# A depthwise convolution moved whole to TensorE, and GpSimd's products and splits moved to VectorE

## The chip, the core and the metric

One core of one Trainium2 chip runs the whole program. Its engines work side by side, each through its own queue in order: TensorE (PE in the profile; its weight loads are PEld), VectorE (DVE), ScalarE (ACT), GpSimd (POOL) and SyncE (SP), which issues most DMAs. The metric is the time of one execution in device microseconds.

## The reference

A network of four blocks, 512 tokens (T) by 1024 features (D = 8 tiles of 128), in float32. The change is in the first half of the first block, "even": an input projection of 5120 columns whose parts feed an S5 layer (a state space recurrence) and a convolution branch, each gated, then an output projection. The convolution branch:

```python
def conformer_conv(val, gate, w_dw, b_dw, ln_g, ln_b, w_pw, b_pw):
    h = val * sigmoid(gate)
    h = depthwise causal convolution of h with w_dw, 31 taps for each channel, + b_dw
    h = silu(layer_norm(h, ln_g, ln_b))
    return h @ w_pw + b_pw
```

(shortened to its steps). The S5 layer expands its poles into powers, keeps 64 groups of states and runs a recurrence over the tokens; the kernel does it by chunks of 8 tokens.

## The kernel before, in words

Features lie on the 128 partitions, the 512 tokens on the free axis. The program is six stages; `stage_even` is the first, from 0 to about 735 us of the trace. Each product is of float32 operands split into a high and a low part (`K.split`: the high part by ScalarE, line L227, the low part by a subtraction, L230, on VectorE unless `eng` names another engine) and takes three passes (`K.passes`, L271, L272, L273). A block of `K.linear`, 128 output columns, loads its weights (`wraw`), splits them into `whi` and `wlo`, and multiplies 8 tiles in three passes, 24 products of 128x512.

Within `stage_even` a scheduler sets the order on each engine from its own model of the times; the order in the source only limits it. The work is:

- The first 8 blocks of the input projection give S5 its inputs. `s5_tables` prepares S5's poles on VectorE meanwhile. The weights' low parts of these 8 blocks are made by GpSimd (`eng=nc.gpsimd`).
- `s5_group`, 8 calls with 4 rounds each: a round makes two sums of two products (`t1`, `t2` into `Gm`; `w1`, `w2` into `w1`), of which VectorE makes the first product and the sum (L685, L687, L693, L695) and GpSimd the second product (L686, L694). TensorE uses them (L700, L701, L709) and ScalarE copies the states into `H`.
- `s5_scan`, 63 steps of four operations on VectorE (L743 to L746); `s5_chunks` (L731) and `s5_outputs` (L761, L763).
- For each of 8 channel tiles `conv(j)`: a gate block (`g`, sigmoid into `sg`), a value block (`v`), `hb` = value times `sg` (L842), and the convolution of the 31 taps into `c`, which GpSimd adds to `acc` and sends to `cv_dr`. Tiles 0 to 3 multiply each tap on ScalarE (L853) and add on GpSimd (L854). Tiles 6 and 7 use a fused multiply and add on VectorE (L860), after the scan. Tiles 4 and 5 run on TensorE (`conv_pe`): the tap's weights become diagonal matrices (`dgh`, `dgl`, by VectorE, L825), and each tap is three products of 128x512 with `hb` shifted, 93 for a tile.
- 16 blocks with silu go to `z_dr`. Then S5's gelu and GLU (8 blocks, `ya`), the layer norm of the convolution, the pointwise layer (8 blocks) and the output projection (8 blocks over 16 tiles).

`CONV_ORDER` lists in which order the tiles and the two halves of the 16 silu blocks stand in the source.

Of the kernel before, what the change touches and what calls it, by code (L numbers as in the profile page):

```python
# [13 lines left out]
F32 = mybir.dt.float32  # L14
# [3 lines left out]
AF = mybir.ActivationFunctionType  # L18
OP = mybir.AluOpType
# [11 lines left out]
# ---------------------------------------------------------------------------  # L31
# host side: layouts only
# ---------------------------------------------------------------------------
# [7 lines left out]
def _blocks_tok(w):  # L41
    """Blocks for products with tokens on the output partitions: [n/256, k half, 128, 4*256]."""
    k, n = w.shape
    return np.ascontiguousarray(
        w.reshape(2, 4, 128, n // 256, 256).transpose(3, 0, 2, 1, 4)
    ).reshape(n // 256, 2, 128, 1024)
# [7 lines left out]
class Layout:  # L54
    """Named columns of the packed per-feature vectors."""
# [16 lines left out]
def host_layout(i):  # L72
# [30 lines left out]
    # block 2  # L103
# [17 lines left out]
    # block 3  # L121
# [23 lines left out]
# ---------------------------------------------------------------------------  # L145
# device side
# ---------------------------------------------------------------------------
# [4 lines left out]
class Ctx:  # L152
# [50 lines left out]
    # -- psum ------------------------------------------------------------  # L203
    def banks(self, es, **split):
        """Share the 8 banks among tags; the tiles of one tag are handed out in order."""
# [14 lines left out]
    # -- exact operand splits ---------------------------------------------  # L220
    def split(self, hi, lo, x, scale=None, eng=None):
        """eng: the engine of lo, or the engines of hi and lo."""
# [18 lines left out]
    def weights(self, src, kt=KT, eng=None, raw=None, pool=None):  # L241
        """One block of up to 128 output columns: [128, kt, 128], split."""
# [8 lines left out]
    def fetch(self, w, blocks, more=(), own=False):  # L251
        """Weights of the first products of the next stage; those of more not split yet.

        own: in a pool of their own, which the next stage closes.
        """
# [10 lines left out]
    def passes(self, ps, terms, first=True, last=True):  # L266
        """terms: (lhs hi, lhs lo, rhs hi, rhs lo); first, last: where the accumulation group starts and ends."""
# [7 lines left out]
    def linear(self, w, blocks, xh, xl, epi, kt=KT, eng=None, front=0, tail=0):  # L275
        """outT[n, t] for each 128-column block of w; epi(j, psum); eng splits the weights.

        The first and the last blocks (front, tail) take one half of the tokens after the other.
        The last ones have epi(j, psum, tokens) and are left to the function returned, of the tokens.
        """  # L280
# [34 lines left out]
    def linear_steps(self, w, blocks, xh, xl, epi):  # L315
        """linear() in steps of KT products of a block."""
# [9 lines left out]
    def linear_tok(self, w, blocks, xh, xl, epi, eng=None):  # L326
        """out[t, n]: tokens on partitions; epi(j, t-pair, psum [128, 2, 256])."""
# [14 lines left out]
    # -- statistics over features ------------------------------------------  # L342
    def colsum(self, s):
        """Sum over partitions, on every partition."""
        ps = self.ax_ps()[:, :s.shape[1]]
        self.nc.tensor.matmul(ps, self.ones, s, start=True, stop=True)
        return ps

    def exp_ln(self, after=None):
        """Load the table set that serves both Exp and Ln."""  # L350
# [3 lines left out]
    def rsqrt(self, *args, load=True, **kw):  # L354
        """out = (scale * ps + eps) ** -0.5, or max(ps, eps) ** -0.5; one Newton step on exp(-ln/2)."""
# [26 lines left out]
    def scratch(self, k, ts, tag):  # L382
        """Room for what is worked out of tile k of x: at the end of a stage, what the stage leaves unused."""
# [13 lines left out]
    def sumsq_ps(self, ps, x, k, ts):  # L397
        """ps accumulates the sum of squares over the features of KT tiles, on every partition."""
# [10 lines left out]
    # -- the ends of stages, in steps between which the halves of the tokens take turns -------  # L409
    def rms_pre(self, g):  # L410
        """What a stage that begins with an RMS norm does with x: its split, scaled by rstd * g."""
# [11 lines left out]
    def modulate_pre(self, scale, shift):  # L423
        """What a stage that begins with a modulation does with x: the split of xt * scale + shift."""
# [10 lines left out]
    def enter(self, xt, pre):  # L435
        """The operands of a stage's first products, unless the stage before has left them."""
# [11 lines left out]
    def leave(self, xt, sums, rest, post, pre, dead, mu=None, first=()):  # L448
        """rest(tokens) and the steps of post(tokens) end a stage, pre begins the next."""
# [18 lines left out]
    def rms_post(self, y, acc, xt, g, sums=None):  # L468
        """xt += rms(y) * g; sums[tokens] = sum of squares of the new xt."""
# [23 lines left out]
class Small:  # L493
    """Arithmetic on small float32 tiles [128, 64]."""
# [88 lines left out]
CONV_POOL = (0, 1, 2, 3)  # L583
CONV_PE = (4, 5)
CONV_ORDER = (0, 1, 6, (0, 8), 2, 3, 7, 4, 5, (8, 16))


def s5_tables(K, pool, R8, J8):
    """Discretised poles, their powers with the signs of each half of the partitions, B bar.

    Partitions are (h, n): h = 0 holds real parts of the states, h = 1 imaginary parts.
    """
# [6 lines left out]
    with K.tc.tile_pool(name="s5sm", bufs=1, side="right", reuse_waits="tile") as sp:  # L599
# [54 lines left out]
        # factors of one chunk for the states and for their copy with the halves swapped  # L654
# [6 lines left out]
def s5_inputs(K, u, A_dr, g0):  # L661
    """u: the inputs of the groups from g0 on, a chunk's rows on partitions."""
# [7 lines left out]
def s5_group(K, tb, p1, rot, g0, u, H, G_dr, K_dr):  # L670
    """GH groups: matrices of a chunk of 8 (inputs to states and to outputs), the states each chunk adds."""
# [6 lines left out]
    for b in range(0, GH, NB):  # L678
# [7 lines left out]
        nc.gpsimd.tensor_tensor(out=t2, in0=pv(tb["Q2"]), in1=cv(1), op=OP.mult)  # L686
# [7 lines left out]
        nc.gpsimd.tensor_tensor(out=w2, in0=pw(tb["Q"]), in1=bv(tb["bbi"]), op=OP.mult)  # L694
# [1567 lines left out]
```

## Time and profile before

| | us |
|---|---|
| median of three runs | 4425.62 (4425.51 to 4428.34) |
| span of the profiled execution, 54533 instructions | 4432.6 |
| of it: TensorE busy | 4120.0 (93%) |
| VectorE busy | 2799.4 (63%) |
| ScalarE busy | 1756.8 (40%) |
| GpSimd busy | 994.4 (22%) |

The profiled execution has no time of its own beside its span; the span is 0.16% above the median. Over the span TensorE is the busiest engine, but these shares are means over six stages. The stage that the change touches is the first, and there the shares differ from stretch to stretch: halves of the first products to 45 us, S5's tables to 83, S5's groups to 204, the scan to 375, S5's outputs and the rest of the projection to 503, the GLU to 551, the pointwise layer from 555.

### The profile page before, as it was taken

To read this page: it belongs to the slowest core of one execution; us is meant where nothing else is said; L and a number is where in the kernel's file an instruction comes from. 1 tells how busy PE (TensorE), PEld (TensorE's weight loads), DVE (VectorE), ACT (ScalarE), POOL (GpSimd) and SP (SyncE) were. 2 spreads that over 40 slices of the span, in tenths; PEclk is the share of its full clock that TensorE was granted. 3 is DMA by queue.
4 is the path that set the end of the run, shared out by engine and by line. 5 is a ranking of instruction groups with operands and counts; after the bars stand their busy time and mean duration, and the time that the engine had idled before them with its cause. 6 is when DMAs were issued, how large, how long until landed. Compare 5 with 4: busy or idle time off the path is not lost.

```text
span 4432.6 us, 54533 instructions
## 1 busy us (share of the span) xinstructions
PE 4120.0 (93%) x20700; PEld 3400.4 (77%) x20700; DVE 2799.4 (63%) x4731; ACT 1756.8 (40%) x2785; POOL 994.4 (22%) x827
## 2 busy tenths in 40 slices
PE   7867897999999899989999999999999999999998
PEld 5656676777776687778888888888877788877887
DVE  8999735555544699997665444444445878735334
ACT  3643634343435522334322322223264444444333
POOL 4855201111021334774000000000023222211000
PEclk9888998999999899999999999999999999999999
DMA  5543533334321123445664434333334222343322
GB/s 149 117 118 116 169 105 117 124 121 136 114 77 53 54 85 127 168 173 202 207 195 140 132 115 128 116 122 119 105 115 149 64 79 70 93 139 109 99 95 86
DMA packets 275062, 532.36 MB, mean 120 GB/s; under 512 B 75968, under 2 KB 149568, under 8 KB 271184
## 3 DMA queue, kind: packets, MB, share of 16 engines
q1 hardware_dynamic: 263328, 505.75, 35.6%
q10 hardware_dynamic: 9216, 9.97, 0.7%
q0 software_dynamic: 2256, 13.17, 0.7%
q8 instruction: 162, 2.65, 0.2%
q14 instruction: 100, 0.82, 0.1%
HBM read 438.11 MB, written 90.70 MB: 119 GB/s over the span
## 4 chain that ended last, share of the span: by engine, by line
PE 49%; DVE 14%; issue 4%; ACT 2%; DMA 2%; POOL 2%; DVEq 0%; SPq 0%; POOLq 0%; ACTq 0%
PE mm L271 14%; PE mm L272 14%; PE mm L273 14%; DVE wlo L230 1%; DVE oa L1500 1%; PE ax L1506 1%; PE z L1225 1%; DVE ti L1435 1%; DVE oe L1501 1%; POOL oe L1502 1%; PE ck L2031 1%; DVE bi L1451 1%; DVE ts L1433 1%; DMA h<-H_dr 1%; DVE wz L1983 0%
## 5 line engine op out<-in xcount | busy, mean ns | idle before, releaser
L271 PE MATMUL mm<-uh,whi 128*128 128x512 f32 (+1 forms) x2888 | 1155.3, 401 | 60.1 <-ACT whi L227 27.0
L273 PE MATMUL mm<-uh,wlo 128*128 128x512 f32 (+1 forms) x2888 | 1131.9, 392 | 53.3 <-DVE wlo L230 49.8
L272 PE MATMUL mm<-ul,whi 128*128 128x512 f32 (+1 forms) x2888 | 1132.3, 392 | 11.3 <-DVE ul L230 9.1
L227 ACT ACTIVATE whi<-wraw 128x1024 fp32r<-128x1024 f32 x455 | 480.3, 1057 | 917.5 <-PE mm L272 650.7
L230 DVE TENSOR_TENSOR wlo<-wraw,whi 128x1024 fp32r<-128x1024 f32 x399 | 515.3, 1293 | 516.5 <-ACT whi L227 504.6
L271 PEld LDWEIGHTS mm<-uh,whi 128*128 128x128 f32 x2888 | 562.8, 195 | 175.6 <-ACT whi L227 31.7
L273 PEld LDWEIGHTS mm<-uh,wlo 128*128 128x128 f32 x2888 | 562.0, 195 | 169.1 <-DVE wlo L230 57.1
L272 PEld LDWEIGHTS mm<-ul,whi 128*128 128x128 f32 x2888 | 563.1, 195 | 120.6 <-DVE ul L230 13.5
L272 PE MATMUL mm<-pl,vh 128*128 128x512 f32 (+1 forms) x1056 | 405.0, 384 | 1.4 <-DVE pl L230 1.4
L273 PE MATMUL mm<-ph,vl 128*128 128x512 f32 (+1 forms) x1056 | 397.7, 383 | 0.0
L271 PE MATMUL mm<-ph,vh 128*128 128x512 f32 (+1 forms) x1056 | 392.8, 384 | 1.9 <-ACT ph L227 1.6
L227 ACT ACTIVATE vh<-wraw 128x1024 fp32r<-128x1024 f32 x128 | 133.1, 1058 | 520.0 <-PE mm L272 320.0
L230 DVE TENSOR_TENSOR vl<-wraw,vh 128x1024 fp32r<-128x1024 f32 x128 | 155.5, 1223 | 190.3 <-ACT vh L227 190.1
L1608 POOL COPY acc<-xt 128x256 f32<-128x256 f32 x2 | 1.9, 961 | 1118.9 <-DVE xt L1606 1118.9
L1603 DVE TENSOR_TENSOR Y<-mm,Y 128x512 f32<-128x512 f32 (+1 forms) x256 | 164.1, 669 | 135.5 <-PE mm L273 135.4
L271 PEld LDWEIGHTS mm<-ph,vh 128*128 128x128 f32 x1056 | 199.2, 189 | 41.1 <-ACT ph L227 1.8
L272 PEld LDWEIGHTS mm<-pl,vh 128*128 128x128 f32 x1056 | 199.2, 189 | 40.8 <-DVE pl L230 2.1
L273 PEld LDWEIGHTS mm<-ph,vl 128*128 128x128 f32 x1056 | 199.3, 189 | 38.7
L1502 POOL TENSOR_TENSOR oe<-oe,sT 128x1024 f32<-128x1024 f32 x64 | 176.5, 2760 | 92.9 <-DVE oe L1501 58.0
L854 POOL TENSOR_TENSOR cvtp<-cvtp,cq 128x512 f32<-128x512 f32 x120 | 174.6, 1456 | 98.6 <-ACT cq L853 93.3
L230 POOL TENSOR_TENSOR wlo<-wraw,whi 128x1024 fp32r<-128x1024 f32 x56 | 154.9, 2771 | 165.7 <-ACT whi L227 165.6
L1506 PEld LDWEIGHTS ax<-oe,oa 128*128 128x128 f32 x1024 | 128.1, 195 | 45.6 <-POOL oe L1502 34.2
(1071 smaller groups left out, 7378.1 us busy)
## 6 DMA issues: line engine op xcount, KB each, us to landing
wraw<-in_peer_u_dram SPq DMA_DIRECT2D x128, 512.0 KB, 3.4
wraw<-in_peer_v_dram SPq DMA_DIRECT2D x128, 512.0 KB, 3.5
wraw<-in_w_in_f_dram SPq DMA_DIRECT2D x66, 512.0 KB, 3.3
G_dr<-st SPq DMA_DIRECT2D x16, 2048.0 KB, 7.5
gt<-G_dr SPq DMA_DIRECT2D x32, 1024.0 KB, 6.8
wraw<-in_w_ffn_dram SPq DMA_DIRECT2D x64, 512.0 KB, 3.3
wraw<-in_w_ada_dram SPq DMA_DIRECT2D x48, 512.0 KB, 3.3
wraw<-in_ev_w_in_dram SPq DMA_DIRECT2D x40, 512.0 KB, 3.4
```

Source lines behind the costliest of these rows:

```text
L227: nc.scalar.activation(out=hi, in_=x, func=AF.Copy)
L230: eng.tensor_tensor(out=lo, in0=x, in1=hi.bitcast(F32), op=OP.subtract)
L271: nc.tensor.matmul(ps, ah, bh, start=first and j == 0, stop=False)
L272: nc.tensor.matmul(ps, ah, bl, start=False, stop=False)
L273: nc.tensor.matmul(ps, al, bh, start=False, stop=last and j == n - 1)
L854: nc.gpsimd.tensor_tensor(out=c, in0=c, in1=t, op=OP.add)
L1225: nc.tensor.matmul(ps[b][:, 128 * (c - b):n], ntri if c == b else nones, at(sp, c, wide[c]), start=False, stop=c == 3, skip_group_check=True)
L1433: v.max(out=ts_[:, x, a:b], in_=src[:, x])
L1435: v.max_index(out=ti[:, x, a:b], in_max=ts_[:, x, a:b], in_values=src[:, x])
L1502: nc.gpsimd.tensor_tensor(out=e, in0=e, in1=sT[:, 2, t0:t0 + 8, None].to_broadcast(sh), op=OP.mult)
L1506: nc.tensor.matmul(pg[:, (r % 4) * 128:(r % 4 + 1) * 128], a[:, r], e[:, r], start=True, stop=True)
L1603: tt(out=Y[:, m, ts], in0=ps, in1=Y[:, m, ts], op=OP.add)
```

## The change

All eight tiles of the convolution run on TensorE by diagonal matrices. The diagonals of eight taps are made by one multiplication of 128x1024 (the last ones of a tile of 128x896), with the identity repeated over the taps and the taps' weights repeated over the columns, instead of eight of 128x128. `hb` has one buffer, in the pool of `conv_pe`; its low split, the taps' low split and the zeroes ahead of it are made by VectorE instead of GpSimd. The second products in `s5_group` and the low splits of the first 8 blocks' weights go to VectorE as well. `CONV_ORDER` puts eight silu blocks first.

```diff
-CONV_POOL = (0, 1, 2, 3)
-CONV_PE = (4, 5)
-CONV_ORDER = (0, 1, 6, (0, 8), 2, 3, 7, 4, 5, (8, 16))
+CONV_ORDER = ((0, 8), 0, 1, 2, 3, 4, 5, (8, 16), 6, 7)
...
         tt(out=t1, in0=pv(tb["P2"]), in1=cv(0), op=OP.mult)
-        nc.gpsimd.tensor_tensor(out=t2, in0=pv(tb["Q2"]), in1=cv(1), op=OP.mult)
+        tt(out=t2, in0=pv(tb["Q2"]), in1=cv(1), op=OP.mult)
...
-        nc.gpsimd.tensor_tensor(out=w2, in0=pw(tb["Q"]), in1=bv(tb["bbi"]), op=OP.mult)
+        tt(out=w2, in0=pw(tb["Q"]), in1=bv(tb["bbi"]), op=OP.mult)
...
-            K.linear(w, range(0, 8), uh, ul, epi_a, eng=nc.gpsimd, front=2)
+            K.linear(w, range(0, 8), uh, ul, epi_a, front=2)
...
-            K.split(wt[0], wt[1], K.v("conv_w", j, 241)[:, ::8], eng=nc.gpsimd)
-            K.split(hs[0], hs[1], hb, eng=nc.gpsimd)
+            K.split(wt[0], wt[1], K.v("conv_w", j, 241)[:, ::8])
+            K.split(hs[0], hs[1], hb)
...
                 for a, b in zip(dg, wt):
-                    for q in range(n):
-                        nc.vector.tensor_scalar(out=a[:, q], in0=K.ident, scalar1=b.bitcast(F32)[:, q0 + q:q0 + q + 1],
-                                                scalar2=None, op0=OP.mult)
+                    sh = [128, n, 128]
+                    nc.vector.tensor_tensor(out=a[:, :n], in0=K.ident[:, None, :].to_broadcast(sh),
+                                            in1=b.bitcast(F32)[:, q0:q0 + n, None].to_broadcast(sh), op=OP.mult)
...
         def conv(j):
-            kind = "p" if j in CONV_POOL else "e" if j in CONV_PE else "v"
-            P = R if kind == "p" else PE
-            hb = P.tile([128, T + 30], F32, name="hb" + kind, bufs=1 if kind == "e" else 2)
-            nc.gpsimd.memset(hb[:, 0:30], 0.0)
+            hb = PE.tile([128, T + 30], F32, name="hb")
+            nc.vector.memset(hb[:, 0:30], 0.0)
...
-            c = P.tile([128, T], F32, name="cvt" + kind, bufs=1 if kind == "e" else 2)
-            if j in CONV_PE:
-                conv_pe(j, hb, c)
-            elif j in CONV_POOL:
-                act(out=c, in_=hb[:, 0:T], func=AF.Identity, scale=K.v("conv_w", j), bias=K.v("conv_b", j))
-                for q in range(1, 31):
-                    t = R.tile([128, T], F32, name="cq")
-                    act(out=t, in_=hb[:, q:q + T], func=AF.Copy, scale=K.v("conv_w", 8 * q + j))
-                    nc.gpsimd.tensor_tensor(out=c, in0=c, in1=t, op=OP.add)
-            else:
...
+            c = PE.tile([128, T], F32, name="cvt", bufs=2)
+            conv_pe(j, hb, c)
```

The rest of the diff takes out comments, so the lines of the changed kernel have lower numbers: the products and sums of `s5_group` are L683 to L693, the scan L741 to L744, the diagonals L822, `hb` L837.

TensorE, the head of a tile on diagonals. In the kernel before, where tile 4's convolution begins (`mm_3303` is its value block, `mm_3338` its convolution, `mm_3514` the next gate block):

```order
L273 MATMUL mm_3303<-uh_75,wlo_3300 128x512
L271 MATMUL mm_3338<-hbh_3330,dgh_3339 128x512
L271 MATMUL mm_3514<-uh_75,whi_3510 128x512
L272 MATMUL mm_3514<-ul_76,whi_3510 128x512
L273 MATMUL mm_3514<-uh_75,wlo_3511 128x512
```

The same place in the changed kernel (`mm_3213`, `mm_3248` and `mm_3370` are the same three):

```order
L273 MATMUL mm_3213<-uh_75,wlo_3210 128x512
L271 MATMUL mm_3248<-hbh_3240,dgh_3249 128x512
L271 MATMUL mm_3370<-uh_75,whi_3366 128x512
L272 MATMUL mm_3370<-ul_76,whi_3366 128x512
L273 MATMUL mm_3370<-uh_75,wlo_3367 128x512
```

The head is as it was: the first diagonal product stands directly behind the value block's last one. What moved is the number of such heads, from two to eight; at tiles 2, 4, 5, 6 and 7 it looks like this, and at tiles 0, 1 and 3 some of S5's short products stand between.

VectorE, a piece of the scan. Before, where `hb` of tile 4 is made (`H_241` holds the states, `sa` and `sb` are the scan's scratch):

```order
L743 TENSOR_TENSOR sa_1799<-H_241,R8_242 128x128
L744 TENSOR_TENSOR sb_1800<-H_241,J8_243 128x128
L745 TENSOR_TENSOR sa_1799<-H_241,sa_1799 128x128
L842 TENSOR_TENSOR hbe_3262<-mm_3303,sg_3264 128x512
L746 TENSOR_TENSOR H_241<-sa_1799,sb_1800 128x128
```

In the changed kernel, where `hb` of tile 2 is made:

```order
L741 TENSOR_TENSOR sa_1763<-H_241,R8_242 128x128
L742 TENSOR_TENSOR sb_1764<-H_241,J8_243 128x128
L743 TENSOR_TENSOR sa_1763<-H_241,sa_1763 128x128
L837 TENSOR_TENSOR hb_2794<-mm_2835,sg_2796 128x512
L744 TENSOR_TENSOR H_241<-sa_1763,sb_1764 128x128
```

The scan stands alike; it is another tile's gating that stands in it, since the tiles on diagonals come earlier.

VectorE, the S5 groups. Before, where `Gm_1070` is filled (`facP` are powers of the poles, `s5cc` and `bbr` S5's output and input matrices):

```order
L687 TENSOR_TENSOR Gm_1070<-t1_1105,t2_1106 128x288
L693 TENSOR_TENSOR w1_1110<-facP_247,bbr_252 128x2x128
L685 TENSOR_TENSOR t1_1121<-facP2_249,s5cc_251 128x288
L693 TENSOR_TENSOR w1_1126<-facP_247,bbr_252 128x2x128
L695 TENSOR_TENSOR w1_1110<-w1_1110,w2_1111 128x2x128
```

In the changed kernel (`Gm_989` is filled there):

```order
L683 TENSOR_TENSOR t1_992<-facP2_249,s5cc_251 128x288
L691 TENSOR_TENSOR w1_997<-facP_247,bbr_252 128x2x128
L684 TENSOR_TENSOR t2_1009<-facQ2_250,s5cc_251 128x288
L685 TENSOR_TENSOR Gm_989<-t1_992,t2_993 128x288
L693 TENSOR_TENSOR w1_997<-w1_997,w2_998 128x2x128
L683 TENSOR_TENSOR t1_1008<-facP2_249,s5cc_251 128x288
L692 TENSOR_TENSOR w2_1014<-facQ_248,bbi_253 128x2x128
```

A round has six operations on VectorE where it had four; a second product stands a round ahead of the sum that uses it (`t2_1009` ahead of the sum of `t2_993`).

More of the change, by code (lines that the diff above doesn't have):

```diff
@@ L745, in s5_scan @@
         tt(out=a, in0=H[:, c], in1=a, op=OP.add)
-        last = tt(out=H[:, c], in0=a, in1=b, op=OP.add)
-    return last
+        tt(out=H[:, c], in0=a, in1=b, op=OP.add)
 def s5_outputs(K, rot, q, H, G_dr, Y1_dr, Y_dr):
@@ L802, in stage_even @@
                 s5_group(K, tb, p1, rot, q * GH, u[:, (q * GH) % (G5 // 2):], H, G_dr, K_dr)
-        scan = s5_scan(K, tb, rot, H)
+        s5_scan(K, tb, rot, H)
         with ExitStack() as s7:
@@ L845, in conv @@
             K.linear(w, [16 + j], uh, ul, epi_v)
-            c = P.tile([128, T], F32, name="cvt" + kind, bufs=1 if kind == "e" else 2)
-            if j in CONV_PE:
-                conv_pe(j, hb, c)
-            elif j in CONV_POOL:
-                act(out=c, in_=hb[:, 0:T], func=AF.Identity, scale=K.v("conv_w", j), bias=K.v("conv_b", j))
-                for q in range(1, 31):
-                    t = R.tile([128, T], F32, name="cq")
-                    act(out=t, in_=hb[:, q:q + T], func=AF.Copy, scale=K.v("conv_w", 8 * q + j))
-                    nc.gpsimd.tensor_tensor(out=c, in0=c, in1=t, op=OP.add)
-            else:
-                with K.tc.issue_after(scan.ins):
-                    nc.vector.tensor_scalar(out=c, in0=hb[:, 0:T], scalar1=K.v("conv_w", j),
-                                            scalar2=K.v("conv_b", j), op0=OP.mult, op1=OP.add)
-                for q in range(1, 31):
-                    nc.vector.scalar_tensor_tensor(
-                        out=c, in0=hb[:, q:q + T], scalar=K.v("conv_w", 8 * q + j),
-                        in1=c, op0=OP.mult, op1=OP.add)
+            c = PE.tile([128, T], F32, name="cvt", bufs=2)
+            conv_pe(j, hb, c)
             if not first:
```

## The prediction

> **What bounds the kernel now.** The change lies in the first of six stages, so I read the trace by stretches of that stage first, then the groups of instructions by line, the shortest, middle and longest instance of single lines, and one piece of the timeline. The span and the stretches (columns: start and end, length, busy time of TensorE's products, its weight loads, VectorE, ScalarE and GpSimd with the number of instructions, the granted clock, the DMA share, GB/s):
>
> ```profile
> span 4432.6 us, 54533 instructions
> 0.00:45.00 45.00, 19.66 (x102) 16.35 (x102) 33.53 (x102) 20.32 (x44) 13.67 (x19) 0.96 0.45 161
> 45.00:83.00 38.00, 34.21 (x142) 27.41 (x142) 37.23 (x80) 8.67 (x13) 17.40 (x9) 0.96 0.46 125
> 83.00:204.00 121.00, 108.50 (x549) 79.25 (x550) 110.94 (x141) 74.84 (x99) 95.55 (x96) 0.89 0.52 119
> 204.00:375.00 171.00, 114.28 (x499) 93.15 (x497) 165.73 (x305) 75.54 (x109) 104.27 (x81) 0.82 0.47 108
> 375.00:450.00 75.00, 62.40 (x291) 53.05 (x291) 74.62 (x128) 22.83 (x32) 40.79 (x27) 0.82 0.53 153
> 503.00:555.00 52.00, 47.18 (x197) 36.48 (x196) 38.72 (x50) 36.13 (x46) 11.68 (x7) 0.99 0.46 157
> 600.00:650.00 50.00, 50.00 (x219) 40.87 (x218) 18.37 (x21) 18.96 (x25) 0.00 (x0) 1.00 0.28 95
> ```
>
> From 45 to 450 us VectorE is busy nearly all the time and TensorE is not: in 204:375, the scan, it lacks 57 of 171 us. From 503 on TensorE is dense. A dense product of 128x512 takes 50.00/219 = 0.228 us; in the GLU's stretch 47.18/197 = 0.239.
>
> VectorE's time is itself stretched. Shortest, middle and longest instance of lines on VectorE (ns):
>
> ```profile
> L743 DVE TENSOR_TENSOR sa<-H,R x63: 277/292/1837, 204.0 to 373.4; 128x128 f32<-128x128 f32 x63
> L685 DVE TENSOR_TENSOR t<-facP,s5cc x32: 443/847/3249, 82.7 to 188.2; 128x288 f32<-128x288 f32 x32
> L687 DVE TENSOR_TENSOR Gm<-t,t x32: 443/450/1546, 83.7 to 190.5; 128x288 f32<-128x288 f32 x32
> L695 DVE TENSOR_TENSOR w<-w,w x32: 410/863/2489, 84.6 to 191.5; 128x256 f32<-128x256 f32 x32
> L230 DVE TENSOR_TENSOR wlo<-wraw,whi x42: 1209/1218/2416, 87.4 to 553.5; 128x1024 fp32r<-128x1024 f32 x42
> ```
>
> The timeline at 340 us shows what stretches them (start, length, engine, line):
>
> ```profile
> 339.60 4.08 POOL L854 TENSOR_TENSOR cvtp<-cvtp,cq 128x512 f32<-128x512 f32 x3
> 341.05 1.31 DVE L743 TENSOR_TENSOR sa<-H,R 128x128 f32<-128x128 f32 x1
> 344.19 0.29 DVE L743 TENSOR_TENSOR sa<-H,R 128x128 f32<-128x128 f32 x1
> 344.40 0.28 DVE L744 TENSOR_TENSOR sb<-H,J 128x128 f32<-128x128 f32 x1
> 344.80 0.68 DVE L842 TENSOR_TENSOR hbe<-mm,sg 128x512 f32<-128x512 f32 x1
> 345.52 0.66 ACT L227 ACTIVATE hbh<-hbe 128x542 fp32r<-128x542 f32 x1 [3.69 <-DVE hbe L842]
> 346.23 0.80 PE L271 MATMUL mm<-hbh,dgh 128*128 128x512 f32 x1 [6.26 <-ACT hbh L227]
> ```
>
> While GpSimd runs its three additions (339.6 to 343.7) the scan's operation takes 1.31 us, behind them 0.29. So VectorE and GpSimd shut each other out on such operations, and GpSimd's work is paid twice. The last three rows are the head of a convolution on TensorE: product, GLU gate, high split, first diagonal product, in one line.
>
> **What the change removes.** Groups (busy us, mean ns | idle before, by releaser):
>
> ```profile
> L854 POOL TENSOR_TENSOR cvtp<-cvtp,cq 128x512 f32<-128x512 f32 x120 | 174.6, 1456 | 98.6 <-ACT cq L853 93.3
> L853 ACT ACTIVATE cq<-hbp,vecs 128x512 f32<-128x512 f32 x120 | 84.3, 717 | 111.0 <-POOL cvtp L854 60.8 <-DVE dgh L825 28.2 <-DMA Tm<-K_dr 10.6
> L860 DVE SCALAR_TENSOR_TENSOR cvtv<-hbv,vecs,cvtv 128x512 f32<-128x512 f32 x60 | 55.1, 944 | 0.0
> L825 DVE TENSOR_SCALAR dgl<-ident,wtl 128x128 fp32r<-128x128 f32 x62 | 25.2, 464 | 0.0
> L825 DVE TENSOR_SCALAR dgh<-ident,wth 128x128 fp32r<-128x128 f32 x62 | 22.7, 427 | 0.4 <-PE mm L272 0.4
> L230 POOL TENSOR_TENSOR wlo<-wraw,whi 128x1024 fp32r<-128x1024 f32 x8 | 21.2, 2668 | 32.2 <-ACT whi L227 32.2
> L686 POOL TENSOR_TENSOR t<-facQ,s5cc 128x288 f32<-128x288 f32 x32 | 29.2, 913 | 20.5 <-DVE w L695 13.1 <-DVE facQ L648 7.4
> L694 POOL TENSOR_TENSOR w<-facQ,bbi 128x256 f32<-128x256 f32 x32 | 26.5, 829 | 6.9 <-DVE Gm L687 6.7
> L273 PE MATMUL mm<-uh,wlo 128*128 128x512 f32 x424 | 177.7, 420 | 40.3 <-DVE wlo L230 40.2
> ```
>
> GpSimd loses 174.6 + 21.2 + 29.2 + 26.5 = 252 us, ScalarE 84 us; VectorE loses 55.1 + 25.2 + 22.7 = 103 us, and the shutting out.
>
> **What it adds.** *VectorE, S5:* the 64 products at the uncontended price of their neighbours, 0.443 and 0.410: 27 us. A group of four then takes 3×0.443 + 3×0.410 = 2.56 us, 32 of them 82 us. *VectorE, weight splits:* 8 at 1.22, 10 us. *VectorE, diagonals:* 64 instructions, 56 of 128x1024 and 8 of 128x896; no row has this form with repeated operands, the nearest is the split L230 of the same size, 1.22 us (0.29 per 128x128 as in the scan's rows would give 8×0.29 = 2.3 us): 64×1.2 = 77 us, at most 150; I take 77, since the S5 rows with repeated operands (L685, 443) cost the same as those without (L687, 443). All told VectorE has some 370 us of work in the first 550: not the bound.
> *TensorE:* six tiles more by diagonals, 6×31×3 = 558 products at 0.228 = 127 us, all on the path now, since TensorE is the bound from the scan on. *Low splits of the tiles on VectorE* cost nothing: their first product stands 26 others (5.9 us) behind the head, and 0.7 us fit; uncovered it would be 0.7 a tile, 6 in all. *The single buffer of hb and of its splits* costs nothing either: a tile's last diagonal product stands 22 products (5 us) ahead of the next tile's head; uncovered, the head comes those 5 us later. *The other order of the blocks* moves the same products. *DMAs* are the same in number, and GpSimd issues them with less ahead of them; *ScalarE's and GpSimd's* remaining work hides under TensorE's.
>
> **The sum.** *To the end of the S5 groups* (204.0 before, where the scan starts). TensorE's order has 384 products of 128x512 and 320 short ones there after the halves, which end by 45 us. Short ones back to back:
>
> ```profile
> 219.67 3.76 PE L731 MATMUL ax<-u,Tm 128*128 128x64 f32 x32
> ```
>
> 0.117 each. Dense: 45 + 384×0.228 + 320×0.117 = 170. VectorE: tables to 76 (83 less some 17 of POOL's 17.4 in 45:83, plus 8×1.22), groups 82, eleven splits 13: 171. Both need each other in turn, so it can't be as short as either; I take 183, between 171 and 195 (half of the saving lost). Saving 21.
>
> *To the GLU.* Behind this stand 528 products of the input projection and 8×93 = 744 of the convolution, 1272×0.228 = 290, and 256 short ones, 30: 320 us if dense, so 503.
>
> *Heads of the convolutions.* By the timeline rows, from the end of the last projection product to the first diagonal one pass 0.68 + 0.66 and some 0.3 between, 1.65 us, whatever else is free, where the head stands directly behind its projection: tiles 2, 4, 5, 6, 7. Tile 0's diagonals stand on VectorE behind the scan's start, which waits for ScalarE's last states (before, 7.7):
>
> ```profile
> DVE sa L743 <- ACT H L713: 7.7, 1, 7.7
> PE mm L271 <- ACT hbh L227: 12.9, 2, 6.7
> ```
>
> I take 5 for it; tile 1's gate has 17 of the scan's operations ahead of it (3), tile 3's two outputs of S5 (2): 5×1.65 + 10 = 18. Two heads cost 12.9 before, so 18 for eight is no high price; the bounds are 8 and 35. Behind each waiting product the whole of TensorE's queue stands, the next tile's gate block first. Gelu's table loads on ScalarE between tiles 4 and 7 delay a high split: 3.
>
> *GLU and the norm.* 8×24×0.239 = 46 us, so it ends at 503 + 18 + 3 + 46 = 570, before at 550.5. The norm of the convolution's output starts with its last tile; before:
>
> ```profile
> 493.60 0.68 ACT L829 ACTIVATE cvte<-mm,vecs 128x512 f32<-128x512 f32 x1
> 534.01 0.69 DVE L957 TENSOR_TENSOR cv<-cv,rstd 128x512 f32<-128x512 f32 x1
> 555.01 1.22 PE L271 MATMUL mm<-uh,whi 128*128 128x512 f32 x2 [4.39 <-ACT uh L227]
> ```
>
> 40.4 us, then silu and split (1.5): 42. In the new order 166 of the GLU's products stand behind the last tile's, 166×0.239 = 40 us: the norm gets no more room than its length, so the wait of 4.4 becomes about 6. First product of the pointwise layer: 576 against 555.0. Nothing behind it changes. So **+21 us**, of it +127 products, −106 of waits and of half speed. Against the profiled span of 4432.6 this is 4453.6; the page gives no time beside the span, so I add the difference to the median of the runs, 4425.62 (0.16% less): **4446.6**.
>
> A page of the Trainium skill bears on the product's price ("TensorE: Matmul & The Clock Gate", section "Wait — 56ns, not 53.3ns?"): N/2.4 GHz + 2.5 ns, 215.7 ns at N = 512. By it the 1272 products would take 16 us less, and the forecast would be about +5, a case of "no change" below. The densest stretch measured has 228, so that chance gets nothing from it.
>
> **The rivals.** *Faster (waits vanish).* With no wait at all: 170 + 320 + 46 = 536, 4.4 of the norm behind: 541, 14 us less than before. It falls on this side only if all of TensorE's waits from 45 on stay under 5 us (−9); taken at 4: 4416. Against it: two heads alone waited 12.9, and a head can't cost less than 1.65. *No change*, within 0.2% or 8.9 us, about what a measurement can tell: waits of 5 to 23 us in all (I forecast 35); taken at 15, 4427. For it: ScalarE and GpSimd are nearly free. *The interlock.* VectorE runs in order; a diagonal waits for TensorE to free one of two buffers, and the scan, a gate or a weight split stands behind it; TensorE waits for that. Row L273 shows the form: 40 us of waits for low splits, in spells up to 13. Half of it coming back: +22 more, 4469. *The clock.* The 0.82 of 204:450 stays: 290×(1/0.82 − 1) = 64 more, 4511. Against it: that stretch had a third of TensorE's time empty, and where it is full the rows have 0.99 and 1.00. The same page of the skill ("What's actually happening") has the clock halve after an idle window of about 3.4 us: with heads of 1.65 us full speed would hold, which takes nothing from my sum; the rows 503:555 and 600:650 agree. *The change doesn't do what it says:* the instructions do move, so I give it nothing.
>
> **How the numbers follow.** Forecast (between 8.9 and 33 more) 0.55, interlock 0.18, no change 0.17, faster 0.05, clock 0.05. The likeliest gives the time; its own range is 4435 to 4458. The range goes from the middle of "no change", 4428, to past the interlock, 4480; left out are faster, clock, and part of "no change". Faster 0.05, same 0.17, slower 0.78.
>
> **What would show it.** In the changed profile: the scan's L741 with median and longest near 0.29 us, its 63 steps ending well ahead of TensorE's convolutions; the last S5 group near 183; a granted clock of 0.95 or more from 200 on; TensorE busy above 90% from 200 to 570; gaps of 1.6 to 5 us at the eight first diagonal products, put down to ACT hbh; L822 at 1.2 us each; the first pointwise product near 576. The prediction is wrong if the gaps behind hbh and the diagonals sum to under 10 or over 35 us, if the groups end before 172 or after 195, or if products cost other than 0.228.

## The result and the profile after

The changed kernel takes 4475.98 us (median of four runs, 4474.16 to 4480.7), the kernel before 4426.98 (4425.51 to 4429.62): 1.0115 times as long, 95% interval 1.0102 to 1.0127, or 49 us more. The forecast was 21 more with a range up to 4480: the direction and the bound are right, the size is off by more than half. That 4475.98 still lies inside the range is luck: the part of it above 4458 was there for the interlock, which did not occur.

The span and the stretches of the profile after (columns as above: length, TensorE's products, its weight loads, VectorE, ScalarE, GpSimd, granted clock, DMA share, GB/s):

```profile
span 4474.3 us, 55137 instructions
45.00:83.00 38.00, 37.53 (x163) 30.72 (x162) 34.09 (x96) 9.94 (x13) 0.00 (x0) 0.99 0.58 148
83.00:183.00 100.00, 94.96 (x535) 70.77 (x535) 81.06 (x198) 59.86 (x79) 8.01 (x9) 0.98 0.69 156
204.00:375.00 171.00, 159.46 (x725) 133.49 (x725) 111.08 (x273) 26.07 (x37) 6.64 (x8) 0.90 0.52 129
375.00:450.00 75.00, 73.53 (x319) 59.63 (x318) 34.15 (x35) 21.27 (x26) 3.60 (x4) 1.00 0.24 84
450.00:503.00 53.00, 51.46 (x226) 42.06 (x225) 14.36 (x14) 14.17 (x18) 0.00 (x0) 1.00 0.28 95
555.00:610.00 55.00, 42.96 (x167) 32.70 (x166) 39.36 (x53) 39.25 (x54) 10.71 (x7) 0.88 0.36 124
```

The roles have changed hands as forecast. From 45 us on TensorE is full, but for two places: somewhere in 204:375 the clock is down to 0.90 on average, and behind 555 there is a hole. VectorE, which had 165.73 of 171 us in the scan's stretch, has 111.08, and from 375 to 503 it is more than half idle. Single lines on VectorE (shortest, middle, longest, ns):

```profile
L741 DVE TENSOR_TENSOR sa<-H,R x63: 281/291/293, 180.9 to 308.6; 128x128 f32<-128x128 f32 x63
L683 DVE TENSOR_TENSOR t<-facP,s5cc x32: 441/451/459, 77.7 to 169.3; 128x288 f32<-128x288 f32 x32
L693 DVE TENSOR_TENSOR w<-w,w x32: 407/418/424, 81.3 to 170.7; 128x256 f32<-128x256 f32 x32
```

The longest instance is now as short as the middle one: with GpSimd's additions and products gone, nothing stretches these lines any more. The scan's longest was 1837 ns, now 293.

Where TensorE waits, in the timeline (start, length; in brackets the idle time before it and what ended it):

```profile
182.76 0.77 PE L271 MATMUL mm<-hbh,dgh 128*128 128x512 f32 x1 [5.04 <-DVE dgh L822]
195.78 3.76 PE L729 MATMUL ax<-u,Tm 128*128 128x64 f32 x32 [0.66 <-DMA Tm<-K_dr]
...
228.82 7.06 PE L729 MATMUL ax<-u,Tm 128*128 128x64 f32 x32 [4.29 <-issue]
...
237.07 6.92 PE L729 MATMUL ax<-u,Tm 128*128 128x64 f32 x32
...
370.74 0.79 PE L271 MATMUL mm<-hbh,dgh 128*128 128x512 f32 x1 [3.60 <-ACT hbh L227]
...
596.26 1.22 PE L271 MATMUL mm<-uh,whi 128*128 128x512 f32 x2 [9.15 <-ACT uh L227]
```

The same 32 short products (L729) take 3.76 us at 195.78 and 7.06 at 228.82. The second time they stand behind a wait of 4.29 us, and the granted clock of that piece says the rest:

```profile
224.00:246.00 22.00, 17.71 (x75) 16.57 (x74) 12.61 (x47) 4.10 (x6) 0.00 (x0) 0.57 0.42 97
```

What they wait for stands on SyncE's queue:

```profile
205.47 5.22 SPq L663 DMA_DIRECT2D u<-A_dr  x8
210.73 13.19 SPq L724 DMA_DIRECT2D Tm<-K_dr  x8
```

Sixteen issues, 18.4 us long, for the second half of `s5_chunks`. They begin at 205.47, when the first half's 64 products (two blocks of 32, 195.78 to 205.4) have read the single buffers `u6` and `Tm`; the last is issued at 224, and TensorE, in order, has reached the products before it lands.

The half speed can outlive the wait by far; what differs is what follows. Behind the wait of 5.04 us at 182.76 come products of 128x512, and their starts are 0.43 us apart for 3 us only. Behind the 4.29 us come the short ones, with three products of 128x512 between their two blocks, and the half speed lasts from 228.8 to 247.4, until products of 128x512 have run for some 4 us in a row (from 243.75).

To compare executions I use, beside the times, the start of the output projection's last half block, since what follows is the same code in every kernel here:

```profile
685.64 0.28 PE L271 MATMUL mm<-uh,whi 128*128 128x256 f32 x1
```

in the kernel before, and in the changed one

```profile
728.11 0.28 PE L271 MATMUL mm<-uh,whi 128*128 128x256 f32 x1
```

42.5 us later. What comes behind this mark took 3736 to 3749 us in the eighteen profiles of this case, with the same instructions: a scatter of some 6 us either way that no part of this change explains. Below, "the mark" is this start.

### The profile page after: what moved, and what is told of

It reads as the page before. It is cut to its first block, busy times and chain, and to the rows that moved or that the text cites. A ratio compares the mean times of both kernels' runs of the same rounds, so it can differ in the third digit from the quotient of the medians.

```text
span 4474.3 us, 55137 instructions
## 1 busy us (share of the span) xinstructions
PE 4224.3 (94%) x21258; PEld 3491.0 (78%) x21258; DVE 2673.8 (60%) x4705; ACT 1678.2 (38%) x2675; POOL 740.3 (17%) x623
## 4 chain that ended last, share of the span: by engine, by line
PE 49%; DVE 14%; issue 4%; DMA 2%; POOL 2%; ACT 2%; SPq 0%; DVEq 0%; POOLq 0%; ACTq 0%
PE mm L271 14%; PE mm L272 14%; PE mm L273 14%; DVE oa L1480 1%; DVE wlo L230 1%; DVE oe L1481 1%; PE ax L1486 1%; PE z L1205 1%; DVE ti L1415 1%; PE ck L2011 1%; POOL oe L1482 1%; DVE bi L1431 1%; DVE ts L1413 1%; DVE eq L1445 0%; DMA h<-H_dr 0%
## 5 line engine op out<-in xcount | busy, mean ns | idle before, releaser
L272 PE MATMUL mm<-ul,whi 128*128 128x512 f32 (+1 forms) x2888 | 1125.6, 390 | 11.6 <-DVE ul L230 11.1
L230 DVE TENSOR_TENSOR wlo<-wraw,whi 128x1024 fp32r<-128x1024 f32 x407 | 515.9, 1269 | 553.9 <-ACT whi L227 541.8
L273 PEld LDWEIGHTS mm<-uh,wlo 128*128 128x128 f32 x2888 | 556.6, 193 | 126.2 <-DVE wlo L230 14.9
L230 DVE TENSOR_TENSOR vl<-wraw,vh 128x1024 fp32r<-128x1024 f32 x128 | 155.5, 1223 | 198.2 <-ACT vh L227 198.2
L1486 PE MATMUL ax<-oe,oa 128*128 128x128 f32 x1024 | 132.9, 281 | 32.5 <-POOL oe L1482 28.0
L1481 DVE TENSOR_TENSOR oe<-iot,sT 128x1024 f32<-128x1024 f32 x64 | 157.0, 2458 | 0.0
```

Of the source, the lines that this page charges most:

```text
L230: eng.tensor_tensor(out=lo, in0=x, in1=hi.bitcast(F32), op=OP.subtract)
L272: nc.tensor.matmul(ps, ah, bl, start=False, stop=False)
L273: nc.tensor.matmul(ps, al, bh, start=False, stop=last and j == n - 1)
L1481: nc.vector.tensor_tensor(out=e, in0=io, in1=sT[:, 0, t0:t0 + 8, None].to_broadcast(sh), op=OP.is_equal)
L1486: nc.tensor.matmul(pg[:, (r % 4) * 128:(r % 4 + 1) * 128], a[:, r], e[:, r], start=True, stop=True)
```

## The experiments

**The kernel before, profiled again.**

> The kernel before, profiled once more, to see whether its profiled execution was a typical one: its span of 4432.6 us lies 7 us above the median of the runs, while the changed kernel's span, 4474.3, lies 1.7 us below its median. Theory: the first profiled execution had about 8 us more in its first stage; then this one has a span of 4424 to 4427 and its first pointwise product near 547 instead of 555. Rival: the profile itself stretches this kernel, and the span is 4432 again with 555.

Measured: span 4421.3, time 4423.07, the first pointwise product at 551.0, the mark at 681.4.

```profile
span 4421.3 us, 54533 instructions
...
551.03 1.22 PE L271 MATMUL mm<-uh,whi 128*128 128x512 f32 x2 [4.39 <-ACT uh L227]
```

The theory is half right (the span is under its 4424 to 4427, the first pointwise product later than its 547): the first profiled execution was a long one, by 11.3 us against this one, of which 4.2 lie ahead of the mark and 7.1 behind. The sum was made against a span 7 us over the typical one and then added to the median.

**The S5 part alone, and the change without it.** `s5_only` is the kernel before with these edits, `conv_only` the changed kernel with them undone:

```diff
-        nc.gpsimd.tensor_tensor(out=t2, ...)
+        tt(out=t2, ...)
-        nc.gpsimd.tensor_tensor(out=w2, ...)
+        tt(out=w2, ...)
-            K.linear(w, range(0, 8), uh, ul, epi_a, eng=nc.gpsimd, front=2)
+            K.linear(w, range(0, 8), uh, ul, epi_a, front=2)
```

> The kernel before with the S5 part of the change alone: the 64 products and the low splits of the first 8 weight blocks on VectorE; the convolution stays as it was, with its additions on GpSimd. Theory (GpSimd and VectorE shut each other out, so 77 us of GpSimd's work are paid twice): the S5 groups end at 185 to 195 instead of 200, and the time falls by 5 to 15 us, to 4411 to 4421. Rival (the convolution's 175 us of additions move into the room on GpSimd and shut VectorE out as before, and VectorE now has 37 us more of its own): 4425 to 4440.

Measured: 4420.55, ratio to before 0.9987 (0.9978 to 0.9996). The time is in the theory's range, its reason is not: TensorE's S5 groups end at 217.5 us, not earlier but 17 later, since the convolution's additions still shut VectorE out (as the rival said: 47 of them, 79.5 us, run on GpSimd between 77 and 217 us, where 28 ran before) and VectorE has more to do. The gain is made later, and why is left open.

> The changed kernel with the S5 part undone: the 64 products and the low splits of the first 8 weight blocks back on GpSimd, the convolution of all eight tiles on TensorE. Theory: the S5 groups, which ended at 171 us on VectorE and 177 on TensorE in the changed kernel, end at 190 to 200, all behind is as it was, and the time is 4488 to 4500. Rival (TensorE's own 170 us of products set that end and VectorE's stretch hides beneath): 4472 to 4480.

Measured: 4491.65, ratio 1.0153 (1.0139 to 1.0167), 15.7 above the changed kernel; the mark at 746.7, 18.6 later. The groups end at 188.1 instead of 177.7, and then the first half of the S5 chunks is waited for 13.3 us instead of 0.7. So the S5 part is worth some 16 us where the additions are gone from GpSimd, and 5 where they are not.

**The heads of the convolutions.** The next tile's blocks are put ahead of a tile's convolution, and `hb` has two buffers (`pipe`):

```diff
+        due = None
-        for j in CONV_ORDER:
+        for j in CONV_ORDER + (None,):
...
-                conv(j)
+                hb = conv(j)
+                if due:
+                    conv_out(*due)
+                due = j, hb
```

> The changed kernel with the heads of the convolutions taken away: the gate and value blocks of the next tile stand in the source ahead of the convolution of a tile, and hb has two buffers, so that TensorE has 48 products to do while VectorE and ScalarE make the tile's operands. Theory: the gaps behind the high splits (five of 1.9 to 4.0 us in the changed kernel, and 5.3 at tile 0) go, 11 to 16 us, and the time is 4460 to 4466. Rival (TensorE then waits for the diagonals or for the next tile's operands as long): 4472 to 4480.

Measured: 4454.02, 22 us less than the changed kernel; the mark at 708.3, 19.8 earlier. TensorE's waits between 177 and 570 us in this kernel (us in all, times, longest):

```profile
PE ax L729 <- DMA Tm<-K_dr: 5.1, 1, 5.1
PE ax L729 <- DMA wraw<-in_ev_w_in_dram: 3.7, 1, 3.7
PE mm L271 <- ACT hbh L227: 1.4, 1, 1.4
PE mm L273 <- DVE wlo L230: 0.6, 1, 0.6
```

Of the waits at the heads (9.9 us for high splits, 5.0 for tile 0's diagonals in the changed kernel) 1.4 us is left, but the waits for the chunks' transfers are longer here, so that all waits of this stretch fall from 21.8 to 10.8 us. Of the other 9 us some 4 are speed that shows: products of 128x512 that start 0.43 us apart instead of 0.23 fall from 37 to 16.

**The norm's wait.** `early` puts the last eight silu blocks behind the last tile, one line:

```diff
-CONV_ORDER = ((0, 8), 0, 1, 2, 3, 4, 5, (8, 16), 6, 7)
+CONV_ORDER = ((0, 8), 0, 1, 2, 3, 4, 5, 6, 7, (8, 16))
```

> The changed kernel with the last eight silu blocks behind all eight tiles of the convolution, where they stood ahead of the last two. The norm of the convolution's output can then run beside 192 more products. Theory: the wait of 9.5 us ahead of the pointwise layer is the norm's chain behind the last tile, so it falls to the 4 or so that the last sigmoid and silu take, and the time is 4468 to 4472. Rival (the wait is ScalarE's table loads and splits between the GLU and the pointwise layer, wherever the last tile stands): 4474 to 4478.

Measured: 4465.25, 10.7 less, below the theory's range. The wait falls from 9.15 to 4.39 us as it said, and the mark comes 4.2 earlier; the other 6 us of the difference lie behind the mark, no more than its scatter, and have no cause shown.

**The wait for the S5 chunks.** A first try gave `Tm` and `u6` two buffers (`chunk2`):

```diff
-    Tm = p2.tile([128, G5 // 2, 128], F32, name="Tm")
-    nc.gpsimd.memset(Tm, 0.0)
     for g0 in range(0, G5, G5 // 2):
+        Tm = p2.tile([128, G5 // 2, 128], F32, name="Tm", bufs=2)
+        nc.gpsimd.memset(Tm, 0.0)
...
-        u = p2.tile([128, G5 // 2, 64], F32, name="u6")
+        u = p2.tile([128, G5 // 2, 64], F32, name="u6", bufs=2)
```

> The changed kernel with two buffers instead of one for the inputs and matrices of the S5 outputs within a chunk (u6, Tm), so that the second half's transfers need not wait for the first half's products. Theory: in the changed kernel TensorE waits 4.3 us for them at 224 us, and the granted clock falls to 0.57 for the 22 us behind, where 64 short products take 14.0 us instead of 7.5 and eight long ones 0.43 instead of 0.23; wait and half speed go together, 11 to 13 us, and the time is 4462 to 4466. Rival (the transfers are as late with two buffers, and the wait only moves): 4472 to 4479.

Measured: 4502.73, ratio 1.0177 (1.0163 to 1.0191), 27 slower than the changed kernel. Neither theory nor rival. Now that no buffer holds the second half back, the scheduler places all 128 short products in a row on TensorE right behind the S5 groups, where none of the 32 transfers has landed. The wait, the 128 products behind it and the granted clock there:

```profile
PE ax L729 <- DMA u<-A_dr: 23.4, 1, 23.4
L729 PE MATMUL ax<-u,Tm x128: 421/421/473, 199.4 to 231.9; 128*128 128x64 f32 x128
177.00:225.00 48.00, 20.71 (x95) 20.40 (x96) 38.02 (x154) 5.14 (x8) 6.96 (x2) 0.51 1.17 141
```

The wait is not the whole harm. Behind it all 128 products run at half speed (the middle one takes 421 ns, against 275 in `late` below), at a granted clock of 0.51, and no product of 128x512 stands among them. Presumably the scheduler's model has the transfers land sooner; no run shows that model. The single buffer had kept the two halves apart on TensorE's queue.

The second try leaves the single buffers and puts the second half's products on TensorE behind tile 2's last product (`late`):

```diff
-CONV_ORDER = ((0, 8), 0, 1, 2, 3, 4, 5, (8, 16), 6, 7)
+CONV_ORDER = ((0, 8), 0, "a", 1, 2, "b", 3, 4, 5, (8, 16), 6, 7)
...
+            if j == "a":
+                next(half)
+            elif j == "b":
+                with K.tc.issue_after(K.last.ins):
+                    next(half)
```

(`half` is `s5_chunks` with a `yield` behind each half, `K.last` the last product traced; the S5 outputs follow at "b".)

> The changed kernel with one buffer for the S5 chunks as it was, but the second half's 64 short products placed on TensorE behind the last product of tile 2's convolution (about 276 us), when their transfers, issued by SP until 224 us, have long landed. Theory: the wait of 4.3 us at 224 and the half speed behind it (6.5 us on short products, 1.6 on long ones) go, and the time is 4462 to 4466. Rival (TensorE only waits elsewhere, or the clock falls for another reason): 4473 to 4478.

Measured: 4463.22, 12.8 less; the mark at 714.2, 13.9 earlier. The same piece of time as above, in this kernel:

```profile
224.00:246.00 22.00, 20.53 (x89) 16.38 (x88) 19.57 (x58) 3.42 (x5) 0.00 (x0) 1.00 1.18 157
```

Full clock and 89 products instead of 75. Taking this wait away, with the half speed behind it, brings 13 to 14 us, three times its length. Not all of it is this one place: `late` also has none of the two waits ahead of the S5 outputs (0.68 and 1.20 us, at 319 and 322), and its order brings two more heads of 1.5 us.

**The three together.** `pipe_early` joins the first two repairs, `pel` all three; `all3` had the two buffers of `chunk2` in place of `late`'s order.

> The changed kernel with three waits removed together: the next tile's blocks ahead of a convolution (22 us alone), the last silu blocks behind the last tile (11 alone), two buffers for the S5 chunks (11 to 13 expected). Theory (the waits and the half speed behind them are what the forecast missed; the 558 products on TensorE's path remain): the sum, 4426 to 4438, so about the kernel before and not faster than it. Rival (the three overlap and less than half of the sum is got): 4440 to 4455. A time under 4415 would say that the products themselves are cheaper than 0.228.

Measured: 4474.71. The buffers' 27 us eat up what the others bring.

> The changed kernel with the next tile's blocks ahead of a convolution and the last tile ahead of the last seven silu blocks. Theory (the two waits are in different places): the sum of the two alone, 22 + 11 us, 4440 to 4446. Rival (they overlap): 4450 to 4456.

Measured: 4439.01, but over a wide 4426.84 to 4447.17; the mark at 700.2, 27.9 earlier than in the changed kernel, where the two alone gave 19.8 and 4.2.

> The same with the second half of the S5 chunks placed later as well. Theory: the sum of all three, some 45 us, 4428 to 4436; the change with TensorE's waits taken out is then still no faster than before, since the 558 products stand on the path. A time under 4415 would say that it was only the waits that made the change slow.

Measured: 4436.56, ratio to before 1.0031 (1.0020 to 1.0043); the mark at 692.9, 35.2 earlier, where the three alone gave 37.9, and the time is just above the theory's range. The waits add up, and behind 250 us what is left is TensorE without a gap up to the GLU (ahead of that the first half of the S5 chunks is still waited for 4.8 us, and the norm behind it 4.4):

```profile
250.00:450.00 200.00, 200.00 (x968) 166.87 (x967) 127.23 (x242) 40.13 (x56) 10.74 (x12) 1.00 0.36 116
```

Even so it is slower than the kernel before.

**Fewer tiles on TensorE.** `dve2`, `dve3` and `dve4` are the changed kernel with tiles 6 and 7, 5 to 7, or 4 to 7 on VectorE, by one multiply and add for a tap, after the scan. All three also have the last eight silu blocks behind the last tile, which is `early`'s repair, so that a part of their gain is not the tiles' (`early` alone brought 4.2 us at the mark, 10.7 in time). The edit of `dve3`:

```diff
+CONV_DVE = (5, 6, 7)
+CONV_ORDER = ((0, 8), 0, 1, 5, 2, 6, 3, 7, 4, (8, 16))
...
-            conv_pe(j, hb, c)
+            if dve:
+                with K.tc.issue_after(scan.ins):
+                    nc.vector.tensor_scalar(out=c, in0=hb[:, 0:T], scalar1=K.v("conv_w", j),
+                                            scalar2=K.v("conv_b", j), op0=OP.mult, op1=OP.add)
+                for q in range(1, 31):
+                    nc.vector.scalar_tensor_tensor(
+                        out=c, in0=hb[:, q:q + T], scalar=K.v("conv_w", 8 * q + j),
+                        in1=c, op0=OP.mult, op1=OP.add)
+            else:
+                conv_pe(j, hb, c)
```

> The changed kernel with tiles 6 and 7 back on VectorE by one multiply and add for each tap, after the scan, as they were before. Theory (TensorE is the bound from the scan on, VectorE has room there): 186 products of 0.229 and two heads of some 2 us less, 45 us, so 4424 to 4436. Rival (VectorE's 62 instructions of 0.74 us, 46 us, delay the operands of the tiles on TensorE and the S5 outputs): 4445 to 4470.

> The same with tiles 5, 6 and 7 on VectorE. Theory: 279 products, three heads and some of the norm's wait less, 70 to 78 us, so 4398 to 4410. Rival (VectorE becomes the bound): no faster than with two tiles by more than 8 us.

> The same with tiles 4 to 7 on VectorE. Theory, if TensorE still bounds: 372 products and four heads less, 93 to 103 us, so 4373 to 4390. Rival: VectorE, with 370 us of work in the changed kernel and some 13 more for each tile moved, has four tiles of 23 us to do after the scan's end at 309, and the norm's chain of 42 us behind the last; then the time stays within 8 us of that with three tiles.

Measured: 4425.43, 4388.07 and 4385.12; ratios to before 1.0001 (0.9992 to 1.0010), 0.9919 (0.9905 to 0.9933), 0.9906 (0.9891 to 0.9921). Two tiles are as foretold, three better than foretold: the third tile's 21 us of products are not 37. Some 9 of the rest are short products, which take 38.4 us in `dve2`, half of those of the S5 chunks at half speed behind a wait of 5.0 us, and 29.7 in `dve3`, where that wait is 2.0 and the speed stays full. The two profiled executions lie 9 us above and 9 us below their medians, so the remainder stays open. With the fourth the rival holds: the last taps and the norm's chain behind them set the end. Its taps and TensorE's two waits ahead of the pointwise layer:

```profile
L850 DVE SCALAR_TENSOR_TENSOR cvt<-hbv,vecs,cvt x120: 717/751/1670, 300.9 to 471.5; 128x512 f32<-128x512 f32 x120
...
508.60 2.05 PE L346 MATMUL ax<-acc,ones 128*128 128x512 f32 x2 [18.77 <-DVE acc L395]
517.72 1.22 PE L271 MATMUL mm<-uh,whi 128*128 128x512 f32 x2 [7.07 <-ACT uh L227]
```

TensorE is through with the GLU at 490 and stands still for 26 of the next 28 us.

Then the repairs on top: `dve3pc` and `dve4pc` with `pipe`'s order, the last tile ahead of seven silu blocks and two chunk buffers; `dve3pl` with `late`'s order in place of the buffers.

> Three tiles on VectorE (4388), with the next tile's blocks ahead of a convolution on TensorE, the last tile ahead of the last seven silu blocks, and two buffers for the S5 chunks. Theory: the gaps at the heads there (5.3, 2.3, 6.4, 1.9 us) and the wait at 224 (2.3) go, 16 to 22 us, and the time is 4366 to 4374, the fastest so far. Rival (VectorE's order, in which taps stand between gates, makes TensorE wait elsewhere): 4380 to 4390.

> The same with four tiles on VectorE. Theory: the taps on VectorE end near 470 there, and the norm's chain of 42 us behind them sets the start of the pointwise layer, so it stays at 4378 to 4390 and is slower than with three. Rival (TensorE still bounds): 20 us under three tiles, 4345 to 4354.

> Three tiles on VectorE (4388 us), with the next tile's blocks ahead of a convolution, the last tile ahead of the last seven silu blocks and the second half of the S5 chunks later. Theory: the heads (5.3, 2.3, 6.4, 1.9 us) and the wait at 224 (2.3) go, 14 to 20 us, and the time is 4368 to 4376. Rival (VectorE's taps delay the tiles' operands, and TensorE waits for them): 4384 to 4392.

Measured: `dve3pc` 4405.77 (0.9953, 0.9940 to 0.9967), slower than `dve3` by 18, for `chunk2`'s reason and not the rival's; `dve4pc` 4389.39 (0.9916, 0.9903 to 0.9930), no better than `dve4` and in the theory's range. But it is not slower than with three tiles, as the theory had it, since `dve3pc` was the slower one, and it waits 17.5 us ahead of the S5 chunks' products, so it doesn't show the norm's chain as the only limit. `dve3pl` takes 4377.59 (0.9896, 0.9881 to 0.9910), 46 us under the kernel before in the same session, the fastest here, just above its expected range of 4368 to 4376. Its interval overlaps that of `dve3` (0.9905 to 0.9933), so a gain by the repairs on top of three tiles is likely but not clear of the noise.

## Why the prediction was wrong, point by point

The mechanism was right: the additions gone from GpSimd set VectorE free, the bound passed to TensorE, and 558 products more stood on its path. `dve2` to `dve3` and `pel` show it: taking tiles off TensorE gives the time back, taking every wait away does not. The terms, each against the trace of the changed kernel:

- *End of the S5 groups*, forecast 183: TensorE's last group product ends at 177.7. 5 us better.
- *Long products*, 1272 at 0.228 and the GLU's 46, together 336: from their starts in the trace, without the waits, 349. The pace is 0.229 where it is undisturbed, with a fifth of them at 0.24; 37 products at half speed make 7 of the 13 us.
- *Short products*, 256 at 0.117, 30 us: 37. Half of the S5 chunks ran at half speed.
- *Waits for the S5 chunks' and outputs' transfers*: no term at all. 6.8 us in four waits, of which 4.3 at 224 us.
- *Heads*, 18 and 3 for gelu: 14.9, five for tile 0 as taken, 9.9 for five others; none at tiles 1 and 3.
- *The norm's wait*, 6: 9.15. ScalarE loads tables six times between 574 and 595 us, 1.28 us each, where the norm's root and the GLU's sigmoids take turns.

In sum −5 + 13 + 7 + 7 − 6 + 3 = 19, of the 20 by which the first pointwise product came later, at 596.3 and not at 576; 1 us more is lost between there and the mark. The groups and the heads erred the other way and hid 11 us of what was missed. One count was off without effect: the diagonals are 48 of 128x1024 and 16 of 128x896, not 56 and 8; they take 1.22 and 1.08 us, as priced.

**The step that failed** is "320 us if dense, so 503": I had taken the waits from the heads alone and the short products at their full-speed row. The change empties the stretch behind the S5 groups of other work, so TensorE reaches the chunks' products sooner than SyncE's sixteen issues let them start; and I priced a wait by its length only, though the rows 204:450 of before, with 0.82, said that waits cost clock as well. The trace of before also had a wait of this kind, 11.1 us ahead of the S5 outputs' products (L761), which the sum took for gone. I used the 0.82 for a rival (the clock, +64) and took it as all or nothing. It came in part: 0.57 for 22 us, 0.90 over 204:375. `late`, which mends this place, brings 13 to 14 us, and `pipe`'s gain at the mark exceeds the waits that it takes away by 9. Of the signs that the prediction named, those for being wrong all stayed away (the groups end at 177.7, the waits at the heads are 14.9 us, the undisturbed products cost 0.229): they looked at the heads and not at the transfers. The clock of 0.95 from 200 on did fail, with 0.90 in 204:375.

The second error is the base: "I add the difference to the median". A time lies 1.7 us above its span (4475.99 and 4474.3 for the changed kernel's profiled execution, which is a median one), so the profiled execution of before, with its span of 4432.6, took some 7 us more than the median of 4426.98. Of the 49 us the two spans show 41.7; 20 to 21 of these are what the sum missed, and the base makes the other 7.

*The rivals.* "Waits vanish" was put at 4416. `pel` has hardly any left and takes 4436.56; its first pointwise product stands at 562.2, not 541. My dense count had the S5 groups end at 170, where TensorE's last group product ends at 177.7 in the changed kernel and 181.3 in `pel` (VectorE's part at 171, so that the two take turns): half of the 21 us. Another 5 are the wait for the first S5 chunks. The interlock did not show: the waits for diagonals are 5.0 us, all at tile 0. "No change" needed waits of 5 to 23 us in all, counted against a first pointwise product at 541; by the same count the changed kernel lost 55.

*The clock.* That it halves after an idle window of about 3.4 us ("TensorE: Matmul & The Clock Gate", "What's actually happening" in the Trainium skill) fits the long waits here: behind those of 3.6, 4.3, 5.0 and 9.2 us the pace is 0.43 for a while, and behind the heads of 1.5 us it stays 0.23. It does not cover all of them, and there the measurement decides: behind tile 2's head, 1.77 us at 280.14, the pace is 0.43 from 281.6 to 285.0, and behind the waits of 0.68 and 1.20 us at 319 and 322, with short products around them, it is half until 329.4. The granted clock of these two pieces, and of one that holds two heads of 1.5 us:

```profile
278.00:315.00 37.00, 35.23 (x155) 28.51 (x153) 30.27 (x83) 4.21 (x6) 1.80 (x2) 0.95 0.14 49
315.00:350.00 35.00, 33.12 (x187) 28.96 (x187) 10.32 (x14) 1.60 (x2) 0.00 (x0) 0.90 0.75 197
482.00:520.00 38.00, 34.92 (x151) 27.83 (x150) 16.59 (x17) 5.80 (x8) 1.80 (x2) 1.00 0.10 38
```

Length alone does not decide it among the short ones: in `dve3` a wait of 1.89 us at 280.0 was followed by half speed and one of 1.96 at 226.5 was not. So the forecast was not safe in taking heads of 1.65 us to leave the clock alone. I had held the window against the rival only, and not asked which of my own waits were longer than it. The 215.7 ns of the same page of the Trainium skill ("Wait — 56ns, not 53.3ns?") for a product of 512 was reached in no dense stretch: 0.227 to 0.229 is the best here.

## What to carry to other kernels

Price a wait on TensorE by its length and by the speed behind it, and look at which products follow: 5.0 us ahead of products of 128x512 brought 3 us of half speed, 4.3 us ahead of two blocks of short ones 19 us of it, and taking the latter away brought about three times the wait. When a change makes a stage denser, look for the transfers that the old idle time had hidden, and read their issues on the queue that makes them; a buffer more can make it worse, where it lets TensorE's products move ahead of their data (27 us here). And before moving work to the engine that will be the bound, move only as much as evens out the two: VectorE stood half idle behind the scan, and three of the eight tiles there, with the silu blocks last, made 1.0115 into 0.9919, with the other repairs 0.9896.

## What was not expected of the hardware

Short products of 128x64 follow each other every 0.11 us at full clock and every 0.22 at half (3.76 and 7.06 us for 32 of them, in the same kernel 33 us apart). At full clock a block of 32 of them does not lower it (195.78, 201.76); once it is half, they do not bring it back: it returned 2 to 8 us after products of 128x512 had begun in `pipe`, `pel`, `dve4`, `chunk2` and `all3`. Multiplying with both operands repeated along a free axis costs VectorE no more than without: L822 takes 1.22 us for 128x1024, as the plain subtraction L230 does. Issuing sixteen strided transfers of 32 to 256 KB kept SyncE's queue for 18.4 us, and TensorE waited for what they brought.
